# Gate products of a hybrid mixer layer: latent and context tokens side by side in one operand tile

## The chip, the cores and the metric

The kernel runs on one core of a Trainium2 chip. The metric is device time in microseconds (us) of one execution. TensorE (PE in the profile) multiplies, VectorE (DVE), ScalarE (ACT) and GpSimd (POOL) do the elementwise work, and SyncE (SP) issues most of the transfers. Each engine works through its own instructions in a fixed order.

## The reference

One layer over 256 latent tokens x, with 256 context tokens as a prefix. Both are normalised and modulated (hx, hc) and multiplied by parts of `w_in`:

```python
hc = modulate(rms_norm(h_ctx, norm1_g[l]), mc[0], mc[1])
out_c, s_f, s_b = token_mixer(hc, *mix_args, zero_state, zero_state, not last)
hx = modulate(rms_norm(x, norm1_g[l]), sh1, sc1)
out_x, _, _ = token_mixer(hx, *mix_args, s_f, s_b, True)
x = x + g1 * out_x
x = x + g2 * conv_ffn(modulate(rms_norm(x, norm2_g[l]), sh2, sc2), ...)
return rms_norm(x, final_g)
```

With one layer the context serves only to give the recurrence its starting states s_f and s_b, so of its projections only the gates (zf, zb) and the values v are needed. The latent tokens need the gates, q, v and all other columns: g, the three parts of the short convolution, and the two merging gates. D is 2048, there are 8 heads of 128 channels, and the FFN is 5632 wide. All is float32.

## The kernel before, in words

**Products.** Each float32 operand is split into an upper part and the remainder: `w_hi` (ScalarE) and `w_lo` (VectorE) for the weights, and two planes `[.., 0, :]` (upper) and `[.., 1, :]` (lower) of a tile for the tokens. A product is the sum of three matmuls: low weights by upper tokens, upper weights by upper tokens, upper weights by lower tokens (`mm3`, L117). The latent tokens are in `hx` [128, 16, 2, 256] and the context tokens in `hc`, of the same shape. Where only latent tokens are wanted (`proj`), one matmul of 512 columns moves upper and lower tokens at once, and one of 256 columns multiplies the low weights: 32 + 32 per call with one group of 256 output columns. Where both token sets are wanted (`block_products` with accumulators zacc, `proj_xc` and `proj_xc1` with accumulators acx), `mm3` is called once for hx and once for hc, in 256 columns each, so six matmuls per weight tile and k. zacc are seven accumulators and acx nine, each over 16 k.

**Weights' way.** A chunk of up to 1 MB comes by SyncE's queue into one of four `raw` slots (`wload`). It is split by halves into `w_hi` and `w_lo` (`wsplit`), five buffers each. `h_block` writes hx and hc for two k at a time; the first stage has eight such blocks with products as soon as they are written.

**Order of the work.** The program is written in one sequence; a scheduler places each engine's instructions ahead of time and may move independent work between. What it can move is limited by memory: a tile waits until those that lay in its place are done. After the first stage come four pairs of heads (g = 0 to 3). For each, gates and q, and then `hgrn` (L445 on): logarithms, scans on VectorE, transposes into kdt (L482), the starting state ps0, scores ps over eight levels (each with exponentials on ScalarE, products on VectorE, matmuls on TensorE and a masked copy), then po, the norm with pn, a reciprocal r (L581), and o_n (L582). While a pair's recurrence runs, TensorE works on other products. Accumulators of 512 columns take PSUM pairs of a pool with three buffers (`bank_pair`, psW); those of hgrn come from another with two (psH). A projection's pair is free again when `joined` has copied one half (ScalarE) and added the other (VectorE) into u, z or sg.

**Memory.** hx lies on the left, hc on the right. The recurrence's pools (vp, gp, g2) are on the left. When the gates are done, hc is released (L613), and its place on the right goes to map_ (the modulation accumulator `macc`) and tp (u, z, cv, sg of the projections that follow). Then mg, y_a and y_b come on the left. The following loop over j has four projections each, with `pump`: one chunk of `w_mod` into a raw slot and a multiply-add into macc (L636), which began with a memset on POOL (L632) and a small load of b_mod (L633).

Later stages: the gated merge into mg, `w_o`, the second norm, the FFN (`w_up`, depthwise convolution, `w_down`) and the final norm, all with products from hx or mg.

Of the kernel before, what the change touches and what calls it, by code (L numbers as in the profile page):

```python
# [16 lines left out]
P = 128  # L17
T = 256
# [18 lines left out]
def hybrid_layer_kernel(ctx: ExitStack, tc: tile.TileContext, I, out, dbg=None):  # L37
# [13 lines left out]
    lop = ctx.enter_context(tc.tile_pool(name="lop", bufs=5))  # L51
    hxp = ctx.enter_context(tc.tile_pool(name="hxp", bufs=1))
# [26 lines left out]

    behind_of = []  # L80

    def wsplit(parts, widths=(1024, 1024), raw=None):

        if raw is None:
            raw = wload(parts)
        for i, n in enumerate(widths):
            half = raw[:, 1024 * i:1024 * i + n]
            hi = hip.tile([P, 1024], F32R, name="w_hi", tag="w_hi")
            lo = lop.tile([P, 1024], F32R, name="w_lo", tag="w_lo")
            with ExitStack() as behind:  # L90
                after, sub = behind_of.pop(0) if behind_of else ((), nc.vector)
                for ins in after:
                    behind.enter_context(tc.issue_after(ins.ins))
                nc.scalar.activation(hi[:, :n], half, AF.Copy)  # L94
                sub.tensor_tensor(out=lo[:, :n], in0=half, in1=hi[:, :n].bitcast(F32), op=ALU.subtract)  # L95
            yield hi, lo

    def wviews(parts, kt):

        for i, (hi, lo) in enumerate(wsplit(parts)):  # L100
            hv = hi[:].rearrange("p (k n) -> p k n", k=kt // 2)
            lv = lo[:].rearrange("p (k n) -> p k n", k=kt // 2)
            for k in range(kt // 2):
                yield i * (kt // 2) + k, hv[:, k, :], lv[:, k, :]
# [4 lines left out]
    def split(dst, src):  # L109
        nc.scalar.activation(dst[0], src, AF.Copy)  # L110
        nc.vector.tensor_tensor(out=dst[1], in0=src, in1=dst[0].bitcast(F32), op=ALU.subtract)  # L111
# [106 lines left out]
    junk = hx[:, 0:2].rearrange("p a b c -> p (a b c)")  # L218
# [51 lines left out]
    def load_block(b):  # L270
        return wload([wblock(w_in, b * 256, 2, (1 + d) * AW, (512, 384)[d]) for d in range(2)])
# [4 lines left out]
    def h_block(b, pm):  # L276

        ks = slice(2 * b, 2 * b + 2)
        sm = stp.tile([P, 2, 256], F32, name="sm", tag="sm")
        copied = nc.vector.tensor_copy(sm[:], pm[:])  # L280
        pc = pm[:, 0, 0:8].rearrange("p (s i c) -> p s i c", s=2, i=2)
        for seg in range(2):
            for i in range(2):
                summed = mm(pc[:, seg, i, :], sm[:, seg, i * P:i * P + P], sel[:], seg == 0 and i == 0, seg == 1 and i == 1)
        pair = [[1, 2], [0, 2]]
        nc.vector.tensor_tensor(out=shcol[:, ks, :], in0=pc[:, 0], in1=strided(pb[:], 2 * b, pair), op=ALU.add)
        nc.vector.tensor_tensor(out=gcol[:, ks, :], in0=pc[:, 1], in1=strided(b1[:], 2 * b, pair), op=ALU.add)
        nc.vector.tensor_tensor(out=gcol[:, ks, :], in0=gcol[:, ks, :], in1=strided(pa[:], 32 + 2 * b, pair), op=ALU.mult)
        for i, h in enumerate((hx, hc)):
            ht = stp.tile([P, 2, T], F32, name="ht", tag=f"ht{i}")  # L290
            for k in range(2):
                kk = 2 * b + k
                nc.vector.tensor_scalar(out=ht[:, k, :], in0=xsT[:, kk, 2 * i:2 * i + 2, :].rearrange("p a b -> p (a b)"),
                                        scalar1=gcol[:, kk, i:i + 1], scalar2=shcol[:, kk, i:i + 1], op0=ALU.mult, op1=ALU.add)
            split((h[:, ks, 0, :], h[:, ks, 1, :]), ht[:])
        return copied, summed

    def block_products(b, halves):

        for d, (hi, lo) in enumerate(halves):  # L300
            for n in ((0, 1, 2, 3), (2, 0, 1))[d]:
                for k in range(2):
                    kk = 2 * b + k
                    at = (512, 384)[d] * k + n * P
                    ns = slice(at, at + P)
                    for i, h in enumerate((hx, hc)):
                        mm3(zacc[d, n][:, i, :], lo[:, ns], hi[:, ns], h[:, kk, 1, :], h[:, kk, 0, :], kk == 0 and i == 0, kk == KD - 1)
                yield
# [51 lines left out]
    dump("hc", hc[:].bitcast(F32))  # L360
# [5 lines left out]
    def proj(w, cols, src, kt):  # L366

        accs = [bank_pair("acc") for _ in cols]  # L370
        for c in range(kt // 8):
            for acc, c0 in zip(accs, cols):
                part = list(wviews([wblock(w, c * 1024, 8, c0, 256)], 8))
                for turn in range(2):
                    for k, hv, lv in part:
                        first = c == 0 and turn == 0 and k == 0
                        last = 8 * (c + 1) == kt and turn == 1 and k == 7
                        for n in range(2):
                            if wide_next[0] == (turn == 0):
                                mm(acc[:, n], hv[:, n * P:n * P + P], src[:, 8 * c + k], first, last)  # L380
                            else:
                                mm(acc[:, n, T:2 * T], lv[:, n * P:n * P + P], src[:, 8 * c + k, 0, :], first, last)
                wide_next[0] = not wide_next[0]
        return [acc[:].rearrange("p n (s t) -> p n s t", s=2) for acc in accs]

    def proj_xc(w, cols):
# [3 lines left out]
        for c in range(2):  # L390
            for n, (hi, lo) in enumerate(wsplit([wblock(w, c * 1024, 8, c0, P) for c0 in cols])):
                for k in range(8):
                    kk = 8 * c + k
                    for i, h in enumerate((hx, hc)):
                        mm3(accs[n][:, i, :], lo[:, k * P:k * P + P], hi[:, k * P:k * P + P],
                            h[:, kk, 1, :], h[:, kk, 0, :], kk == 0 and i == 0, kk == KD - 1)
        return accs

    def proj_xc1(w, c0):

        acc = bank_pair("acx")[:, 0].rearrange("p (a b) -> p a b", a=2)
        for k, hv, lv in wviews([wblock(w, 0, KD, c0, P)], KD):
            for i, h in enumerate((hx, hc)):
                mm3(acc[:, i, :], lv, hv, h[:, k, 1, :], h[:, k, 0, :], k == 0 and i == 0, k == KD - 1)
# [24 lines left out]
    def values(cb):  # L429
        pairs = [bank_pair("vacc") for _ in range(2)]  # L430
        accs = [pairs[t // 2][:, t % 2] for t in range(4)]
        for c4 in range(4):
            for k, hv, lv in wviews([wblock(w_in, c4 * 512, 4, 3 * AW + cb * 512, 512)], 4):
                kk = 4 * c4 + k
                for t in range(4):
                    h = hx if t < 2 else hc
                    ts = slice((t % 2) * P, (t % 2) * P + P)
                    mm(accs[t], h[:, kk, 0, ts], hv, kk == 0, False)
                    mm(accs[t], h[:, kk, 0, ts], lv, False, False)
                    mm(accs[t], h[:, kk, 1, ts], hv, False, kk == KD - 1)  # L440
# [3 lines left out]
    def hgrn(g, ft, q):  # L444
# [131 lines left out]
        split((oh[:], ol[:]), osq[:])  # L576
# [52 lines left out]
    def mod_steps():  # L629
        for seg in (4, 3, 2, 5):  # L630
            acc = map_.tile([P, D], F32, name="macc", tag="macc")
# [15 lines left out]
            else:  # L647
                yield
                bc = xp.tile([P, D], F32, name="bc", tag="bc")
                for c, (hi, lo) in enumerate(wsplit(None, raw=acc)):  # L650
                    for n in range(2):
                        cs = slice(n * 512, n * 512 + 512)
                        pm = psH.tile([P, 512], F32, name="pm2", tag="psh")
                        mm(pm[:], ones_r[:], hi[:, cs], True, False)
                        mm(pm[:], ones_r[:], lo[:, cs], False, True)
# [10 lines left out]
    for j in range(4):  # L666
# [19 lines left out]
        split((y_b[:, 2 * j:2 * j + 2, 0, :], y_b[:, 2 * j:2 * j + 2, 1, :]), cv[:])  # L686
# [8 lines left out]
        split((y_a[:, 2 * j:2 * j + 2, 0, :], y_a[:, 2 * j:2 * j + 2, 1, :]), sg[:])  # L695
# [7 lines left out]
    for j in range(8):  # L703
# [13 lines left out]
        split((mg[:, 2 * j:2 * j + 2, 0, :], mg[:, 2 * j:2 * j + 2, 1, :]), mb[0][:])  # L717
# [120 lines left out]
    with tc.manual_schedule(engines={nc.vector.engine}):  # L838
        for k2 in range(KD // 2 + 1):
            if k2 < KD // 2:  # L840
                ks = slice(2 * k2, 2 * k2 + 2)
                nc.vector.tensor_tensor(out=xg[:, ks, :], in0=xg[:, ks, :], in1=rbv, op=ALU.mult)
                for k in range(2 * k2, 2 * k2 + 2):
                    h2_hi[k2] = nc.scalar.activation(hx[:, k, 0, :], xg[:, k, :], AF.Identity, bias=sh2[:, k:k + 1])
            if k2 > 0:
                for k in range(2 * k2 - 2, 2 * k2):
                    h2_lo[k2 - 1] = nc.vector.scalar_tensor_tensor(out=hx[:, k, 1, :], in0=xg[:, k, :], scalar=sh2[:, k:k + 1], in1=hx[:, k, 0, :].bitcast(F32),  # L847
# [5 lines left out]
    mgp_cm.__exit__(None, None, None)  # L853
    onp.__exit__(None, None, None)

# [43 lines left out]
    fg = map_.tile([P, D], F32, name="fg", tag="macc")  # L899
    nc.scalar.dma_start(fg[:], I["final_g"].rearrange("(o d) -> o d", o=1).to_broadcast([P, D]))  # L900

    def y_part(k0):
        ys = hx[:, k0 % KD:k0 % KD + 2]
        split((ys[:, :, 0, :], ys[:, :, 1, :]), y[:, k0:k0 + 2, :])
        return lambda k, p: ys[:, k, p, :]
# [57 lines left out]
```

## Time and profile before

| what | value |
|---|---|
| runs, median (lowest to highest) | 1749.36 us (1749.27 to 1750.08), three runs |
| the profiled execution | 1748.87 us |
| its span, first to last instruction | 1747.1 us |
| mean granted TensorE clock | 0.993 |
| transferred | 384.95 MB, 220 GB/s mean |

The span is the profiled execution without its start and end. In the chain of waits a row gives start, duration, engine, output name and the hardware's count of passes; a float32 matmul that isn't split counts more than one pass, so that 8 ps instructions stand there as 16. In the grouped view a row gives busy time and mean of one in ns; matmuls overlap in the array, so such a mean is longer than the distance between two of them.

### The profile page before, as it was taken

The numbers are of one execution on the slowest core, as the hardware profiler recorded it, in microseconds if no ns is written. First come the engines' busy times: TensorE is split into PE (matmuls) and PEld (weight loads), VectorE is DVE, ScalarE is ACT, GpSimd is POOL, SyncE is SP. The second block draws the span as 40 slices with busy tenths as digits, with TensorE's granted clock in tenths as the row PEclk, the third lists the DMA queues.
The fourth block names the chain that finished last, engine by engine and source line by source line (L and its number), as shares of the span: only waits on it lengthen the run. The fifth ranks groups of instructions, "written<-read, shape, count | busy, mean of one in ns | idle before, by whom it ended". The sixth has DMA issues, their size and how long they took to land.

```text
span 1747.1 us, 25679 instructions
## 1 busy us (share of the span) xinstructions
PE 1712.9 (98%) x10391; PEld 1490.8 (85%) x10391; DVE 1311.7 (75%) x1689; ACT 894.8 (51%) x1141; POOL 20.5 (1%) x26
## 2 busy tenths in 40 slices
PE   5999999999999999999999999999999999999997
PEld 3778888999888888888888788888888888888886
DVE  4437267677998978878875589888888887876774
ACT  4217246565665544444465454444444454765653
POOL 0000000000000000000000000000000000000000
PEclk9999999999999999999999999999999999999999
DMA  9997323232877879989886367777777765656652
GB/s 333 346 331 231 97 73 98 74 120 93 272 258 246 273 266 324 318 275 314 289 304 218 125 199 246 234 235 237 241 241 239 234 202 193 193 193 193 193 193 72
DMA packets 288987, 384.95 MB, mean 220 GB/s; under 512 B 7812, under 2 KB 241581, under 8 KB 280038
## 3 DMA queue, kind: packets, MB, share of 16 engines
q1 hardware_dynamic: 287872, 379.82, 65.8%
q10 hardware_dynamic: 694, 3.24, 0.5%
q8 instruction: 81, 1.33, 0.3%
q14 instruction: 36, 0.29, 0.1%
q0 software_dynamic: 304, 0.26, 0.1%
HBM read 381.20 MB, written 2.10 MB: 219 GB/s over the span
## 4 chain that ended last, share of the span: by engine, by line
PE 97%; DVE 1%; ACT 1%; DMA 0%; issue 0%; SPq 0%; ACTq 0%
PE acc L114 56%; PE to L114 19%; PE acx L114 6%; PE vacc L114 5%; PE zacc L114 5%; PE pm L114 2%; PE ps L114 2%; PE po L114 1%; PE pt L236 1%; DMA xt<-in_x_dram 0%; PE pc L114 0%; DVE w_lo L95 0%; PE kdt L482 0%; ACT sq L789 0%; PE ptx L827 0%
## 5 line engine op out<-in xcount | busy, mean ns | idle before, releaser
L95 DVE TENSOR_TENSOR w_lo<-raw,w_hi 128x1024 fp32r<-128x1024 f32 (+1 forms) x521 | 630.0, 1218 | 226.1 <-ACT w_hi L94 210.4
L94 ACT ACTIVATE w_hi<-raw 128x1024 fp32r<-128x1024 f32 (+1 forms) x522 | 548.0, 1054 | 482.6 <-PE acc L114 316.8
L114 PE MATMUL acc<-hx,w_hi 128*128 128x512 f32 x2560 | 606.3, 392 | 2.3 <-DVE hx L847 2.3
L114 PEld LDWEIGHTS acc<-hx,w_hi 128*128 128x128 f32 x2560 | 476.7, 189 | 98.7 <-DVE hx L847 3.3
L114 PEld LDWEIGHTS acc<-hx,w_lo 128*128 128x128 f32 x2560 | 320.8, 192 | 8.1 <-DVE w_lo L95 0.8
L114 PE MATMUL acc<-hx,w_lo 128*128 128x256 f32 x2560 | 324.7, 283 | 0.1
L114 PE MATMUL to<-w_hi,hx 128*128 128x512 f32 (+1 forms) x792 | 221.5, 365 | 0.0
L636 DVE SCALAR_TENSOR_TENSOR macc<-raw,cst,macc 128x2048 f32<-128x2048 f32 x64 | 150.3, 2348 | 24.2 <-DMA raw<-in_w_mod_dram 18.5
L114 PEld LDWEIGHTS to<-w_hi,hx 128*128 128x128 f32 x792 | 142.8, 188 | 24.4
L114 PE MATMUL to<-w_lo,hx 128*128 128x512 f32 (+1 forms) x396 | 144.9, 366 | 0.0
L882 DVE SCALAR_TENSOR_TENSOR cvf<-av,pf,cvf 128x189 f32<-128x189 f32 (+2 forms) x352 | 129.2, 428 | 1.4 <-ACT cvf L870 1.3
L110 ACT ACTIVATE hx<-y 128x512 fp32r<-128x512 f32 x88 | 55.0, 630 | 87.6 <-PE to L114 86.1
L111 DVE TENSOR_TENSOR hx<-y,hx 128x512 fp32r<-128x512 f32 x88 | 60.7, 692 | 36.7 <-ACT hx L110 36.6
L114 PEld LDWEIGHTS to<-w_lo,hx 128*128 128x128 f32 x396 | 74.6, 188 | 12.2
L114 PE MATMUL to<-w_hi,mg 128*128 128x512 f32 (+1 forms) x288 | 81.1, 367 | 0.0
L114 PE MATMUL acx<-hx,w_hi 128*128 128x256 f32 x288 | 59.7, 286 | 0.0
L114 PEld LDWEIGHTS to<-w_hi,mg 128*128 128x128 f32 x288 | 51.8, 188 | 8.8
L114 PE MATMUL acx<-hc,w_hi 128*128 128x256 f32 x288 | 59.2, 285 | 0.0
L114 PE MATMUL to<-w_lo,mg 128*128 128x512 f32 (+1 forms) x144 | 52.7, 366 | 0.0
L114 PE MATMUL zacc<-hx,w_hi 128*128 128x256 f32 x224 | 49.3, 286 | 0.5 <-DVE hx L111 0.5
L114 PE MATMUL zacc<-hc,w_hi 128*128 128x256 f32 x224 | 47.1, 287 | 0.0
L114 PEld LDWEIGHTS acx<-hx,w_hi 128*128 128x128 f32 x288 | 45.3, 191 | 0.9
(240 smaller groups left out, 1758.6 us busy)
## 6 DMA issues: line engine op xcount, KB each, us to landing
raw<-in_w_up_dram SPq DMA_DIRECT2D x88, 1024.0 KB, 5.2
raw<-in_w_in_dram SPq DMA_DIRECT2D x81, 1024.0 KB, 5.9
raw<-in_w_mod_dram SPq DMA_DIRECT2D x64, 1024.0 KB, 6.7
raw<-in_w_down_dram SPq DMA_DIRECT2D x44, 1024.0 KB, 5.1
raw<-in_w_mod_dram SPq DMA_DIRECT2D x64, 512.0 KB, 6.9
raw<-in_w_o_dram SPq DMA_DIRECT2D x16, 1024.0 KB, 6.1
raw<-in_w_in_dram SPq DMA_DIRECT2D x24, 512.0 KB, 4.4
raw<-in_w_pa_dram SPq DMA_DIRECT2D x8, 1024.0 KB, 5.6
```

Source lines behind the costliest of these rows:

```text
L94: nc.scalar.activation(hi[:, :n], half, AF.Copy)
L95: sub.tensor_tensor(out=lo[:, :n], in0=half, in1=hi[:, :n].bitcast(F32), op=ALU.subtract)
L110: nc.scalar.activation(dst[0], src, AF.Copy)
L111: nc.vector.tensor_tensor(out=dst[1], in0=src, in1=dst[0].bitcast(F32), op=ALU.subtract)
L114: return nc.tensor.matmul(o, lhsT, rhs, start=start, stop=stop, skip_group_check=True)
L236: nc.tensor.transpose(pt[:, k, :], xts[2 * i + t][k4 // 2][:, kk * P:kk * P + P], ident[:])
L636: nc.vector.scalar_tensor_tensor(out=acc[:], in0=raw[:], scalar=cst[:, k, 0:1], in1=acc[:], op0=ALU.mult, op1=ALU.add)
L882: nc.vector.scalar_tensor_tensor(out=c4[:, ro, co], in0=a4[:, ri, ci], scalar=pf[:, tap * NF + f:tap * NF + f + 1], in1=c4[:, ro, co], op0 ...
```

## The change

hx and hc become one tile H [128, 16, 4, 256] with the planes latent low, latent upper, context upper, context low. The upper parts lie side by side (planes 1 and 2) and the lower at the ends (0 and 3). `mm3` takes both token sets at once: two matmuls over planes 1:3, and one over planes 0:4:3, of 512 columns each. hx is now a name for planes 0:2, so latent-only products use the same memory, upper and lower exchanged.

```diff
-    hx = hxp.tile([P, KD, 2, T], F32R)
-
-    hcp_cm = tc.tile_pool(name="hcp", bufs=1, side="right")
-    hcp = hcp_cm.__enter__()
-    hc = hcp.tile([P, KD, 2, T], F32R)
+    H = hp.tile([P, KD, 4, T], F32R)
+    hx = H[:, :, 0:2, :]
...
-    def mm3(o, wl, wh, sl, sh, start, stop):
-
-        mm(o, wl, sh, start, False)
-        mm(o, wh, sh, False, False)
-        mm(o, wh, sl, False, stop)
+    def mm3(o, wl, wh, k, start, stop):
+
+
+        mm(o, wh, H[:, k, 1:3, :], start, False)
+        mm(o, wh, H[:, k, 0:4:3, :], False, False)
+        mm(o, wl, H[:, k, 1:3, :], False, stop)
...
-                    for i, h in enumerate((hx, hc)):
-                        mm3(accs[n][:, i, :], lo[:, k * P:k * P + P], hi[:, k * P:k * P + P],
-                            h[:, kk, 1, :], h[:, kk, 0, :], kk == 0 and i == 0, kk == KD - 1)
+                    mm3(accs[n], part(1, k * P, k * P + P), part(0, k * P, k * P + P), kk, kk == 0, kk == KD - 1)
...
-    hcp_cm.__exit__(None, None, None)
-    map_ = ctx.enter_context(tc.tile_pool(name="map", bufs=1, side="right", reuse_waits="tile"))
+    map_cm = tc.tile_pool(name="map", bufs=1, reuse_waits="tile")
+    map_ = map_cm.__enter__()
     tp_cm = tc.tile_pool(name="tp", bufs=2, side="right", reuse_waits="tile")
     tp = tp_cm.__enter__()
-    mgp_cm = tc.tile_pool(name="mgp", bufs=1, reuse_waits="tile")
-    mgp = mgp_cm.__enter__()
...
-    mg = mgp.tile([P, KD, 2, T], F32R)
+    mg = H[:, :, 2:4, :]
...
+    lop_cm.__exit__(None, None, None)
+    lo_ring += range(KD // 2)
```

What else it moves: mg, which held its own memory, takes the context's planes of H. The pool of low weight halves is released before the FFN; from then on the low halves lie in eight places of H's planes 2 and 3 (`lo_half`). map_ moves to the left, and tp remains on the right, where hc no longer was; the last modulation row and final_g get other tiles. Everything that read hx or hc is rewritten for H.

TensorE's order at the recurrence of head pair 3. Before, from its transposes (kdt) on; ps are the scores, acc the mixer's projections:

```order
1538 L482 MATMUL kdt<-ident,ft 128x128 x8
1539 L114 MATMUL acc<-hx,w_hi 128x512 x20
1540 L114 MATMUL ps_3997<-v,gc 128x128 x8
1541 L114 MATMUL ps<-q,ks 64x64 x8
1542 L114 MATMUL acc<-hx,w_hi 128x512
1543 L114 MATMUL acc<-hx,w_lo 128x256 x28
1544 L114 MATMUL ps<-qe,ke 64x64 x8
1545 L114 MATMUL acc<-hx,w_lo 128x256 x4
1546 L114 MATMUL acc<-hx,w_hi 128x512 x19
1547 L114 MATMUL ps<-qe,ke 64x64 x8
1548 L114 MATMUL acc<-hx,w_hi 128x512 x13
1549 L114 MATMUL acc<-hx,w_lo 128x256 x32
```

It goes on in this way up to pn. Now, from the same transposes on:

```order
926 L491 MATMUL kdt<-ident,ft 128x128 x8
927 L126 MATMUL acc<-H,w_lo 128x256 x4
928 L126 MATMUL acc<-H,w_hi 128x512 x16
929 L126 MATMUL ps_3225<-v,gc 128x128 x8
930 L126 MATMUL ps<-q,ks 64x64 x8
931 L126 MATMUL ps<-qe,ke 64x64 x56
932 L126 MATMUL ps<-qe,ke 128x128 x4
933 L126 MATMUL po<-ft,kt 128x256 x2
934 L126 MATMUL po<-ft,v 128x256 x2
937 L126 MATMUL pn<-oh,ones_r 128x512
938 L126 MATMUL pn<-ol,ones_r 128x512
939 L126 MATMUL acc<-H,w_hi 128x512 x16
```

The projections that stood between the levels now stand behind pn.

VectorE's order around u, the first tile of the mixer's projections (its add frees the first PSUM pair). Before, with the logarithms of head pair 3 (X, gc) still ahead of its scans:

```order
361 L462 TENSOR_TENSOR X_3966<-X_3966,ft_3434 128x1024
362 L463 TENSOR_TENSOR gc_3967<-gc_3967,ft_3434 128x1024
363 L426 TENSOR_TENSOR q_3954<-q_3954,sq_3957 128x512
364 L95 TENSOR_TENSOR w_lo_4351<-raw_4344,w_hi_4350 128x1024
365 L125 TENSOR_TENSOR u_4292<-acc_4207,u_4292 128x512
366 L95 TENSOR_TENSOR w_lo_4404<-raw_4401,w_hi_4403 128x1024
```

Now, with the last step of head pair 3 (ft, ol, r, o_n) and the first two chunks of macc:

```order
416 L572 TENSOR_TENSOR ft_2854<-ft_2854,q_3182 128x512 x2
417 L123 TENSOR_TENSOR ol_3405<-osq_3401,oh_3404 128x512
418 L590 RECIPROCAL r_3410<-r_3410 128x512
419 L644 SCALAR_TENSOR_TENSOR macc_3518<-raw_3521,cst_91,macc_3518 128x2048
420 L591 TENSOR_TENSOR o_n_1101<-po_3392,r_3410 128x512
421 L644 SCALAR_TENSOR_TENSOR macc_3518<-raw_3620,cst_91,macc_3518 128x2048
422 L138 TENSOR_TENSOR u_3515<-acc_3430,u_3515 128x512
423 L138 TENSOR_TENSOR z_3609<-acc_3524,z_3609 128x512
```

u's add went from ahead of head pair 3's scans to behind its o_n.

More of the change, by code (lines that the diff above doesn't have):

```diff
@@ L77, in wload, with lo_half @@
         return raw
+    lo_ring = []
+    def lo_half():
+        if not lo_ring:
+            return lop.tile([P, 1024], F32R, name="w_lo", tag="w_lo")[:].rearrange("p (a n) -> p a n", a=2)
+        i = lo_ring.pop(0)
+        lo_ring.append(i)
+        return H[:, 2 * i:2 * i + 2, 2:4, :].rearrange("p a b t -> p a (b t)")
     behind_of = []
@@ L86, in wsplit @@
         for i, n in enumerate(widths):
-            half = raw[:, 1024 * i:1024 * i + n]
-            hi = hip.tile([P, 1024], F32R, name="w_hi", tag="w_hi")
-            lo = lop.tile([P, 1024], F32R, name="w_lo", tag="w_lo")
+            two = lambda ap: ap.rearrange("p (a n) -> p a n", a=2)[:, :, :n // 2]
+            half = two(raw[:, 1024 * i:1024 * i + 1024])
+            hi = two(hip.tile([P, 1024], F32R, name="w_hi", tag="w_hi")[:])
+            lo = lo_half()[:, :, :n // 2]
             with ExitStack() as behind:
@@ L217, in hybrid_layer_kernel @@
     rstd = sp.tile([P, 4], F32)
[L218 removed]
+    junk = H[:, 0].rearrange("p b c -> p (b c)")
     for i in range(2):
@@ L270, in load_block @@
     def load_block(b):
-        return wload([wblock(w_in, b * 256, 2, (1 + d) * AW, (512, 384)[d]) for d in range(2)])
+        raw = rawp.tile([P, 2, 2, 512], F32, name="raw", tag="raw")
+        for d, n in enumerate((512, 384)):
+            nc.sync.dma_start(raw[:, d, :, :n], wblock(w_in, b * 256, 2, (1 + d) * AW, n)[0])
+        return raw[:].rearrange("p d k n -> p (d k n)")
     def split_block(raw):
@@ L303, in block_products @@
                     kk = 2 * b + k
[L304 to L307, printed above, removed]
+                    at = 512 * k + n * P
+                    mm3(zacc[d, n], part(1, at, at + P), part(0, at, at + P), kk, kk == 0, kk == KD - 1)
                 yield
@@ L381, in proj @@
                             else:
-                                mm(acc[:, n, T:2 * T], lv[:, n * P:n * P + P], src[:, 8 * c + k, 0, :], first, last)
+                                mm(acc[:, n, 0:T], lv[:, n * P:n * P + P], src[:, 8 * c + k, 1, :], first, last)
                 wide_next[0] = not wide_next[0]
@@ L402, in proj_xc1 @@
         for k, hv, lv in wviews([wblock(w, 0, KD, c0, P)], KD):
-            for i, h in enumerate((hx, hc)):
-                mm3(acc[:, i, :], lv, hv, h[:, k, 1, :], h[:, k, 0, :], k == 0 and i == 0, k == KD - 1)
+            mm3(acc, lv, hv, k, k == 0, k == KD - 1)
         return acc
@@ L630, in mod_steps @@
         for seg in (4, 3, 2, 5):
-            acc = map_.tile([P, D], F32, name="macc", tag="macc")
+            acc = map_.tile([P, D], F32, name="macc", tag="macc") if seg != 5 else xp.tile([P, D], F32, name="bc", tag="bc")
             nc.gpsimd.memset(acc[:], 0.0)
@@ L648, in mod_steps @@
                 yield
-                bc = xp.tile([P, D], F32, name="bc", tag="bc")
-                for c, (hi, lo) in enumerate(wsplit(None, raw=acc)):
+                bc = xp.tile([P, D], F32, name="bc", tag="bc") if seg != 5 else acc
+                for c, part in enumerate(wsplit(None, raw=acc)):
                     for n in range(2):
-                        cs = slice(n * 512, n * 512 + 512)
                         pm = psH.tile([P, 512], F32, name="pm2", tag="psh")
-                        mm(pm[:], ones_r[:], hi[:, cs], True, False)
-                        mm(pm[:], ones_r[:], lo[:, cs], False, True)
+                        mm(pm[:], ones_r[:], part(0, n * 512, n * 512 + 512), True, False)
+                        mm(pm[:], ones_r[:], part(1, n * 512, n * 512 + 512), False, True)
                         nc.scalar.copy(bc[:, c * 1024 + n * 512:c * 1024 + n * 512 + 512], pm[:])
```

61 lines of the change are left out of this document (30 added, 31 removed).

## The prediction

> **What bounds the kernel now.** I read the page first: the engine totals, the chain that ended last, the groups.
>
> ```profile
> span 1747.1 us, 25679 instructions
> PE 1712.9 (98%) x10391; PEld 1490.8 (85%) x10391; DVE 1311.7 (75%) x1689; ACT 894.8 (51%) x1141; POOL 20.5 (1%) x26
> PE 97%; DVE 1%; ACT 1%; DMA 0%; issue 0%; SPq 0%; ACTq 0%
> L114 PE MATMUL acx<-hx,w_hi 128*128 128x256 f32 x288 | 59.7, 286 | 0.0
> L114 PE MATMUL zacc<-hx,w_hi 128*128 128x256 f32 x224 | 49.3, 286 | 0.5 <-DVE hx L111 0.5
> ```
>
> TensorE is the bound from end to end. So time can only be won by giving it less to do, and anything that leaves it without work is added to the span. The 98% is an average, so next comes the stretch that the change touches, in the chain of waits: the heads' recurrences (kdt, ps, po, pn) with what runs between.
>
> ```profile
> 168.14 43.52 PE vacc L114 x192
> 338.44 12.84 PE acx L114 x107
> 374.05 0.87 PE kdt L482 x8
> 378.04 2.40 PE ps L114 x32
> 383.51 1.08 PE ps L114 x32
> 389.82 0.62 PE ps L114 x16
> 405.14 0.62 PE ps L114 x16
> 407.50 0.89 PE ps L114 x8
> 411.81 3.02 PE po L114 x14
> 414.83 4.66 PE acx L114 x39
> 421.98 43.36 PE acc L114 x251
> 465.34 0.87 PE kdt L482 x8
> 548.25 3.46 PE po L114 x16
> 559.27 65.78 PE acc L114 x380
> ```
>
> The columns are start, duration, work. Each recurrence is a long serial pass over VectorE with scraps of TensorE work; from kdt (374.05) to the end of po (414.83) head pair 2 takes 40.8 us. TensorE loses nothing by it, because products of other tiles (acx there, acc at head pair 3, from 465.34 on) lie in between.
>
> **The merge itself.** A matmul's duration in the groups (286 ns) overlaps its neighbours'; what counts is the pace. 256 columns: 12.84 us / 107 = 120 ns. 512 columns: 43.52 / 192 = 227 ns. One product over both token sets in place of two saves 2 x 120 - 227 = 13 ns. With w_lo half as many again as w_hi's 288 and 224 for hx alone, there are 432 pairs in acx and 336 in zacc: 5.7 and 4.5 us, 10.2 at most. The Trainium skill's "TensorE: Matmul & The Clock Gate", section "Back-to-back issue gap", gives N / 2.4 + 2.5 ns for a warm matmul, so a fixed cost of only 2.5 ns per matmul: by it the 768 pairs would be worth 2 us, an estimate from that page. The trace's fixed part is five times that, and the trace decides.
>
> For acx I take the whole 5.7 us. For zacc not:
>
> ```profile
> 36.00:157.00 121.00, 120.31 (x957) 94.26 (x958) 50.18 (x99) 32.14 (x42) 0.95 (x1) 0.99 1.00 324
> GB/s 333 346 331 231 97 73 98 74 120 93 272 258 246 273 266 324 318 275 314 289 304 218 125 199 246 234 235 237 241 241 239 234 202 193 193 193 193 193 193 72
> ```
>
> In this stage (us, then PE, PEld, DVE, ACT, POOL busy, clock, DMA share, GB/s) the DMA share is 1.00 too. Its best slice moved 346 GB/s, so 121 us x 324 / 346 = 113 us is the least for the same bytes, and a TensorE gain can be had in part. Also, in the last block VectorE now has three w_lo and the copy of pf ahead of the shift and scale columns on which the last products wait (before, two w_lo, further on). Between 0 and 4.5 I take 3.0, nearer the PE row since TensorE is busy 120.3 of the 121 us.
>
> The low part is now read with stride (two runs of 256 columns). The nearest row of a strided operand is pm's, whose 512 columns are two runs of 256 of raw; the contiguous neighbour is po:
>
> ```profile
> 62.02 0.99 PE pm L114 x8
> ```
>
> Po took 3.46 us for 16 passes of 256 columns, 216 ns each, so 432 for 512; pm's eight passes (four 32-wide groups beside each other, so two in a row) took 0.99, at most 495 with all their overhead. So I price the stride at nothing; its other end, half rate, is a rival below.
>
> **The cover that goes.** H takes the place of hx and hc, and hc's memory on the right, freed once the gates were done, is no longer where u, z and macc are put: they now lie over memory that the recurrence's own pools hold until head pair 3 is finished. The order shown with the change has the result. Before, u of the first mixer projection was added up ahead of head pair 3's kdt:
>
> ```profile
> L125 DVE TENSOR_TENSOR u<-acc,u x4: 686/692/693, 447.3 to 592.4; 128x512 f32<-128x512 f32 x4
> ```
>
> (the first at 447.3, kdt at 465.34), so its PSUM pair came free and eight projections flowed between the levels. Now u stands behind r, macc, o_n and macc of the end of head pair 3; three projections fill the three PSUM pairs, the fourth has no bank, and TensorE's row from kdt on is 20 acc, 76 ps, 8 po, 2 pn and nothing between. Everything behind that fourth projection waits.
>
> How long? From the start of kdt:
> 1. To the end of po: 40.8 us in head pair 2. Only VectorE and ScalarE work counts in it, less what they did for others:
>
> ```profile
> 374.00:415.00 41.00, 22.71 (x79) 14.89 (x78) 6.09 (x5) 0.00 (x0) 1.00 0.24 78
> 415.00:465.00 50.00, 21.32 (x146) 19.51 (x145) 19.38 (x16) 0.00 (x0) 1.00 0.64 215
> ```
>
> (tile w_lo alone: PE, PEld, DVE, POOL). Five w_lo, 6.1 us, give a lower end of 34.7. Four w_lo stay in after's row, behind two weight loads that get a raw slot late, as the w_mod chunks keep three of the four; I take 38, ends 34.7 and 40.8.
>
> 2. From po to the restart, by the rows after head pair 2's po (ACT, then DVE):
>
> ```profile
> 414.93 0.60 ACT L572 ACTIVATE osq<-po 128x512 f32<-128x512 f32 x1 [5.91 <-PE po L114]
> 417.81 0.63 ACT L110 ACTIVATE oh<-osq 128x512 fp32r<-128x512 f32 x1
> 419.41 1.28 ACT L580 ACT_TABLE_LOAD   x1
> 420.71 0.69 ACT L580 ACTIVATE r<-pn,eps_t 128x512 f32<-128x512 f32 x1
> 418.48 0.69 DVE L111 TENSOR_TENSOR ol<-osq,oh 128x512 fp32r<-128x512 f32 x1
> 421.43 3.35 DVE L581 RECIPROCAL r<-r 128x512 f32<-128x512 f32 x1 [0.78 <-ACT r L580]
> 426.65 0.68 DVE L582 TENSOR_TENSOR o_n<-po,r 128x512 f32<-128x512 f32 x1
> 427.25 2.34 DVE L636 SCALAR_TENSOR_TENSOR macc<-raw,cst,macc 128x2048 f32<-128x2048 f32 x1
> ```
>
> 0.60 + 0.63 + 0.69 + two pn 0.46 + table 1.28 + root 0.69 = 4.35 (less where the table load is early), reciprocal 3.35, macc 2.34, o_n 0.68, macc 2.34, u 0.69: 13.7; I take 13.5. Ends 12.5 and 16, the latter with the 9.95 us that lay between po's end and the reciprocal's in the trace. Macc's own new wait hides in it: its memset on POOL now waits for po too, and
>
> ```profile
> L632 POOL MEMSET macc<- 128x2048 f32 x4 | 7.2, 1807 | 480.9 <-PE pc L114 334.3 <-DVE w_lo L95 133.3 <-PE acx L114 13.3
> macc<-in_b_mod_dram POOLq DMA_DIRECT2D x4, 8.0 KB, 1.8
> ```
>
> 1.8 + 1.8 us end well ahead of the reciprocal, 7.5 us behind po. Were it later, u would follow it one for one.
>
> 3. TensorE's own work in this time: kdt 0.87, 20 acc (4 x 0.120 + 16 x 0.227 = 4.1), ps 2.40 + 1.08 + 5 x 0.62 + 0.89 = 7.5, po 3.5, pn 0.5: 16.4 us. So it stands idle 38 + 13.5 - 16.4 = 35.1 us.
>
> Around the hole three smaller terms:
> - Ahead of kdt. From po of pair 2 on, TensorE now has 99 acc of 256 and 96 of 512 columns, 33.7 us, with po and pn 37, up to a kdt that VectorE must have ready.
>
> ```profile
> 415.00:466.00 51.00, 51.00 (x317) 45.94 (x315) 47.49 (x49) 37.26 (x41) 2.34 (x2) 1.00 0.65 218
> ```
>
> Of VectorE's 47.49 us there, 16 w_lo (19.38, quoted above) and a macc were for others: 25.8 without. After's row has 11 w_lo (1.22 each) in this piece: 39. TensorE waits 2 to 5 us; I take 3.
> - The clock. Where TensorE is idle at times, its granted clock falls:
>
> ```profile
> 990.00:998.00 8.00, 6.56 (x44) 5.45 (x42) 3.69 (x11) 3.08 (x11) 0.00 (x0) 1.00 0.00 0
> 998.00:1008.00 10.00, 7.64 (x22) 5.23 (x22) 9.65 (x17) 9.51 (x17) 0.00 (x0) 0.50 0.32 105
> ```
>
> Behind the second norm it was 0.50 for ten us. In the hole that doubles po, 3.5 us on the chain (a level's ps lies beside VectorE's next level), and some us of products after the restart. I take 4, ends 0 and 8. The Trainium skill's "TensorE: Matmul & The Clock Gate", Part 1, has the clock halved after about 3.4 us of idling and full again after as long of work; by it the restart would cost half of 3.4 us, an estimate from that page. The rows agree on the half, but not on the time: ten us there, in which TensorE had work for 7.6.
> - Changes between acc and ps, po that no longer happen: from 466.21 to 559.27 lie 79.7 us of acc by the paces above (233 of 512, 224 of 256 columns) and 11.5 of ps, po and pn, so 1.8 us went to the changes: -1.8.
>
> The rest of TensorE's row (w_o, the FFN, w_down) is in the same order as before; the low halves' places in H have more room than the pool that they replace, and mg's move touches no wait of TensorE. Those edits I cost at nothing; TensorE's back-to-back products cover them, and a late low half would cost at most its 1.22 us at each place. The gate products, being shorter, cover less of the levels of pairs 1 and 2: 0 to 3 us, I take 0.
>
> **Sum.** 35.1 + 3 + 4 - 1.8 = 40.3 lost, 5.7 + 3.0 = 8.7 won. The profiled run took 1748.87 us (1.8 of it outside the span), so 1748.87 + 40.3 - 8.7 = 1780.5; the median of the runs, 1749.36, is 0.5 above that run. Forecast: 1780 us.
>
> **The rivals.**
> - *The cover is kept (faster).* Then only the merge counts: 1748.9 - 8.7 = 1740. It needs u, z and macc free before head pair 3 ends, or other work in TensorE's row. For it: in head pairs 1 and 2 the same recurrence costs TensorE nothing. Against it: engines work their rows in order, u is behind r in VectorE's, and the fourth projection's bank is behind u. It decides if the idle time is under 8.7 us; 16.4 us of work against a serial pass of over 34 leaves no such room. Chance 0.06.
> - *The strided operand runs at half rate.* 112 + 144 low products at 227 ns more would be 58 us on top: 1838. The pm row speaks against it. 0.04.
> - *The durations of the groups are paces.* 2 x 286 less a 512-column matmul's 392, the other reading of the same page, would be 180 ns for each of 768 pairs, 138 us: 1651. Against it, 107 matmuls took 12.84 us and not 30. 0.01.
> - *The merge does not pay and the hole is small*, so that nothing is seen (within 0.2%, 3.5 us, about what a measurement of this kernel tells from no change): 0.03.
>
> The forecast's own case has 0.86. Its range, by the terms' ends: at the low end 34.7 + 12.5 - 16.4 + 2 + 0 - 1.8 - 10.2, or +20.8: 1770. At the high end 40.8 + 16 - 16.4 + 5 + 8 - 5.7 + 3, or +50.7: 1800. Not all ends come together, and some of the chance lies below: 1765 to 1797. Faster 0.07, same 0.03, slower 0.90.
>
> **What would show it.** In the profile after: zacc and acx of 512 columns at 227 ns each, 336 and 432 of them; the first stage about 3 us shorter; from kdt of head pair 3 a stretch of some 50 us in which TensorE is busy for a third, its clock at 0.5, ended by the add into u, and acc from there on without gaps; the idle time before acc put down to VectorE. If that stretch is full of acc, or if u is added up ahead of r, the forecast is wrong; if the span has grown but the hole is under 25 us, the chain was mis-sized.

## The result and the profile after

The changed kernel takes 1780.92 us (median of 4 runs, 1779.8 to 1782.81), the kernel before 1749.72 us beside it; the ratio is 1.0177 with a 95% interval of 1.0159 to 1.0194. Slower, as forecast, by 31.2 us against 31 forecast. The profiled execution took 1780.26 us, its span 1778.5. From the page of the profile after:

```profile
span 1778.5 us, 24106 instructions
PE 1710.1 (96%) x9623; PEld 1454.0 (82%) x9623; DVE 1312.4 (74%) x1689; ACT 890.9 (50%) x1137; POOL 20.6 (1%) x26
PE 91%; DVE 3%; DMA 2%; ACT 2%; issue 1%; SPq 0%; ACTq 0%
```

768 matmuls fewer, and yet TensorE is busy for a smaller share: it now waits. The timeline of TensorE, from kdt of head pair 3 to the fourth projection of the mixer, shows where (start, duration, engine, line, operation, count, and in brackets the idle time before and what ended it):

```profile
459.02 1.04 PE L491 MATMUL kdt<-ident,ft 128*128 128x128 f32 x8
...
468.89 0.69 PE L126 MATMUL ps<-qe,ke 128*64 128x64 f32 x16 [0.52 <-DVE ke L546]
477.17 1.12 PE L126 MATMUL ps<-qe,ke 128*64 128x64 f32 x16 [7.60 <-DVE qe L540]
479.58 1.12 PE L126 MATMUL ps<-qe,ke 128*64 128x64 f32 x16 [1.28 <-DVE qe L540]
482.65 1.12 PE L126 MATMUL ps<-qe,ke 128*64 128x64 f32 x16 [1.95 <-DVE qe L540]
...
492.60 1.67 PE L126 MATMUL po<-ft,kt 128*128 128x256 f32 x4 [0.36 <-DVE ft L572]
...
495.83 1.03 PE L126 MATMUL po<-ft,v 128*128 128x256 f32 x4
498.26 0.49 PE L126 MATMUL pn<-oh,ones_r 128*128 128x512 f32 x1 [1.41 <-ACT oh L122]
...
509.29 2.93 PE L126 MATMUL acc<-H,w_hi 128*128 128x512 f32 x6 [9.79 <-DVE u L138]
```

From the second level on every ps waits for VectorE, and acc comes back only when u has been added up, 9.79 us after pn. The longest wait between levels, 7.60 us, holds a late weight chunk: ScalarE stands for it ahead of the exponentials of that level, and VectorE splits the chunk before it comes to the level's products. ScalarE's row:

```profile
471.44 2.00 ACT L107 ACTIVATE w_hi<-raw 128x1024 fp32r<-128x1024 f32 x2 [3.34 <-DMA raw<-in_w_in_dram]
```

VectorE's timeline ahead of the restart has the row that the order promised:

```profile
500.25 3.35 DVE L590 RECIPROCAL r<-r 128x512 f32<-128x512 f32 x1 [1.31 <-ACT r L589]
503.52 2.25 DVE L644 SCALAR_TENSOR_TENSOR macc<-raw,cst,macc 128x2048 f32<-128x2048 f32 x1
505.69 0.69 DVE L591 TENSOR_TENSOR o_n<-po,r 128x512 f32<-128x512 f32 x1
506.29 2.34 DVE L644 SCALAR_TENSOR_TENSOR macc<-raw,cst,macc 128x2048 f32<-128x2048 f32 x1
508.55 0.68 DVE L138 TENSOR_TENSOR u<-acc,u 128x512 f32<-128x512 f32 x1
```

Three windows of the kernel after (us; then PE, PEld, DVE, ACT, POOL busy; granted clock, DMA share, GB/s):

```profile
459.00:509.30 50.30, 22.16 (x201) 18.23 (x199) 34.06 (x46) 21.63 (x34) 2.33 (x2) 0.71 0.23 77
...
480.00:490.00 10.00, 4.07 (x62) 3.40 (x58) 9.85 (x19) 5.78 (x11) 0.00 (x0) 0.50 0.01 2
...
510.00:520.00 10.00, 10.00 (x52) 8.71 (x51) 9.85 (x9) 3.98 (x5) 0.00 (x0) 0.79 0.86 280
```

In 50.3 us TensorE is busy for 22.2, some of it at half the clock. Before, it was busy all of that time; 50.3 us from kdt on:

```profile
465.34:515.64 50.30, 50.30 (x370) 43.95 (x369) 48.04 (x57) 30.06 (x40) 0.00 (x0) 1.00 0.72 245
```

To see the rest of the account, take the distance from the start of each matmul to the start of the next, and add it up by the name of the output (this divides TensorE's whole time, waits and slow clock included; us):

```
            before     after   difference
ps           29.99     50.94       +20.95
pn            1.85     12.42       +10.57
po           12.31     14.33        +2.02
pm           46.26     49.26        +3.00
pt           20.20     22.44        +2.24
acx         107.61    102.24        -5.37
zacc         87.06     83.51        -3.55
acc         987.99    988.28        +0.29
ptx, vacc, rb, pc, kdt (sum)        +1.06
first to last start                +31.2
```

The hole stands in ps, pn and po: 33.5 us. acx brought what the pace promised. zacc brought 3.55. pm (the modulation's products, between the blocks of zacc) and pt (transposes; the last four stand ahead of the last block's products, so that a wait of 1.62 us for H counts as theirs) took 5.2 back.

### The profile page after: what moved, and what is told of

It is laid out like the page before. It is cut to its first block, busy times and chain, and to the rows that moved or that the text cites. A ratio compares the mean times of both kernels' runs of the same rounds, so it can differ in the third digit from the quotient of the medians.

```text
span 1778.5 us, 24106 instructions
## 1 busy us (share of the span) xinstructions
PE 1710.1 (96%) x9623; PEld 1454.0 (82%) x9623; DVE 1312.4 (74%) x1689; ACT 890.9 (50%) x1137; POOL 20.6 (1%) x26
## 4 chain that ended last, share of the span: by engine, by line
PE 91%; DVE 3%; DMA 2%; ACT 2%; issue 1%; SPq 0%; ACTq 0%
PE acc L126 53%; PE to L126 18%; PE acx L126 6%; PE vacc L126 5%; PE zacc L126 4%; PE pm L126 2%; DMA raw<-in_w_in_dram 1%; PE ps L126 1%; PE po L126 1%; DVE w_lo L108 1%; PE pt L248 1%; DMA xt<-in_x_dram 0%; ACT w_hi L107 0%; PE pc L126 0%; DMA raw<-in_w_mod_dram 0%
## 5 line engine op out<-in xcount | busy, mean ns | idle before, releaser
L126 PE MATMUL acc<-H,w_hi 128*128 128x512 f32 x2560 | 605.3, 393 | 12.1 <-DVE u L138 9.8
L126 PEld LDWEIGHTS acc<-H,w_hi 128*128 128x128 f32 x2560 | 478.7, 190 | 109.6 <-DVE u L138 10.1
L108 DVE TENSOR_TENSOR w_lo<-raw,w_hi 128x1024 fp32r<-128x1024 f32 (+1 forms) x258 | 308.5, 1211 | 146.1 <-ACT w_hi L107 141.7
L108 DVE TENSOR_TENSOR H<-raw,w_hi 128x1024 fp32r<-128x1024 f32 x263 | 319.4, 1220 | 70.7 <-ACT w_hi L107 70.2
L126 PE MATMUL to<-w_hi,H 128*128 128x512 f32 (+1 forms) x1080 | 302.6, 366 | 0.0
L126 PEld LDWEIGHTS to<-w_hi,H 128*128 128x128 f32 x1080 | 194.6, 188 | 33.2
L126 PEld LDWEIGHTS acc<-H 128*128 128x128 f32 x1408 | 175.4, 191 | 5.3 <-DVE H L108 1.6
L126 PE MATMUL acc<-H 128*128 128x256 f32 x1408 | 176.9, 283 | 0.6 <-DVE H L108 0.6
L126 PE MATMUL acc<-H,w_lo 128*128 128x256 f32 x1152 | 146.8, 283 | 0.0
L126 PE MATMUL to<-H 128*128 128x512 f32 (+1 forms) x396 | 144.9, 366 | 0.0
```

Source lines behind the costliest of these rows:

```text
L108: sub.tensor_tensor(out=lo, in0=half, in1=hi.bitcast(F32), op=ALU.subtract)
L126: return nc.tensor.matmul(o, lhsT, rhs, start=start, stop=stop, skip_group_check=True)
```

## The experiments

The theory: the slowdown is the lost cover. u and z lie over memory of the recurrence, so three PSUM pairs fill up and TensorE has nothing to do until head pair 3 is done. Rival 1: the merge itself takes the cover, since shorter gate products leave less to put between the levels. Rival 2: chunks of w_mod, which wait for macc in the raw slots, starve the weights.

**1. late_uz: the wait without the merge.** In the kernel before, only this is added (for u and the first two z, at j = 0):

```diff
-        joined(u[:], pc0)
+        with ExitStack() as late:
+            if j == 0:
+                late.enter_context(tc.issue_after(last_on.ins))
+            joined(u[:], pc0)
```

> The kernel before, gate products unmerged, hx and hc apart; only the adds into u and the first two z are issued behind the last o_n of head pair 3. Theory (the hole comes from the late u and z, not from the merge): TensorE again stands without work from kdt of head pair 3 to the add into u; 50 us less 14 to 16 of its own work gives about 34 us more, 1784 us (1777 to 1790). Rival 1 (the merge itself takes the cover, since shorter gate products leave less to put between the levels): nothing is merged here, so 1750. Rival 2 (the chunks of w_mod hold the raw slots and starve the weights): the accumulator is as free as before, so 1750 to 1755.

Measured: 1778.16 us, ratio 1.0161 (1.0147 to 1.0175). TensorE's window from kdt to the restart, and the restart in its timeline:

```profile
465.50:507.80 42.30, 20.65 (x188) 16.88 (x186) 30.89 (x44) 18.85 (x30) 0.00 (x0) 0.72 0.28 96
```

```profile
507.84 5.50 PE L114 MATMUL acc<-hx,w_hi 128*128 128x512 f32 x16 [5.56 <-DVE u L125]
```

Without any merge the same hole appears, and 27.8 of the 31.2 us with it. It is at the low edge of what was expected for two reasons: no macc stands ahead of u here (5.56 us of idling behind pn in place of 9.79), and the way from kdt to the end of po is 34.3 us in place of 37.9. Rival 1 falls as the cause, and a late u and z are enough.

**2. defer_macc: the chunks of w_mod later.** The changed kernel with

```diff
-        pump(1)
+        pump((0, 2, 1, 1)[j])
```

at all four places of the loop over j.

> The changed kernel with the first four chunks of w_mod put two iterations' worth later (none at j = 0, two at a time at j = 1), so that no macc stands ahead of u on VectorE and no raw slot is held by w_mod in the recurrence. Theory: the hole stays, since u and z still lie over the recurrence's memory; its tail loses two macc (4.7 us) and the 7.6 us that a level waited for a weight load can shrink: 1769 to 1776. Rival 2 (w_mod's raw slots are the cause): most of the 34 us goes, 1745 to 1752. Rival 1 (the merge): 1781.

Measured: 1774.09 us, ratio 1.0136 (1.0122 to 1.015): 6.8 us less than the change. kdt is at 458.74 and the restart at 504.44, 45.7 us in place of 50.3. Behind pn nothing is won, however. TensorE's restart, and VectorE ahead of it:

```profile
504.44 6.45 PE L126 MATMUL acc<-H,w_hi 128*128 128x512 f32 x16 [9.80 <-DVE u L138]
```

```profile
501.44 2.34 DVE L644 SCALAR_TENSOR_TENSOR macc<-raw,cst,macc 128x2048 f32<-128x2048 f32 x1
503.70 0.68 DVE L138 TENSOR_TENSOR u<-acc,u 128x512 f32<-128x512 f32 x1
```

Two macc are still ahead of u: the chunks of j = 1 are as early as that, once TensorE stands. So the edit didn't remove what I said that it would, and what it won lies elsewhere: the longest wait between levels is 3.08 us instead of 7.60.

```profile
471.86 0.78 PE L126 MATMUL ps<-qe,ke 128*64 128x64 f32 x16 [3.08 <-DVE qe L540]
```

The weight loads come earlier: SyncE has issued the last two ahead of the restart by 457.29, where in the change it does so from 457.19 to 466.64. Rival 2 is a part of the loss here, no more.

**3. split: the merge taken back inside the changed kernel.**

```diff
-        mm(o, wh, H[:, k, 1:3, :], start, False)
-        mm(o, wh, H[:, k, 0:4:3, :], False, False)
-        mm(o, wl, H[:, k, 1:3, :], False, stop)
+        for i, (hi, lo) in enumerate(((1, 0), (2, 3))):
+            mm(o[:, i, :], wh, H[:, k, hi, :], start and i == 0, False)
+            mm(o[:, i, :], wh, H[:, k, lo, :], False, False)
+            mm(o[:, i, :], wl, H[:, k, hi, :], False, stop)
```

> The changed kernel with each gate product made again as two of 256 columns, H and the placement of u, z and macc as changed. Theory: TensorE has the 5.7 us of acx back to do, the first stage is longer by up to 2 us, but the order now leaves 10 us of projections in the recurrence of head pair 3 instead of 4, so the sum hardly moves: 1778 to 1785. Rival 1 (the merge is the cause of the hole): 1750 to 1756.

Measured: 1778.16 us, ratio 1.0159 (1.0144 to 1.0175). The hole is there with unmerged products as well. The 6 us more of projections that lie in it and the 5.4 us of acx that come back nearly cancel: by the distances between starts, ps has 7.1 us less than in the change and acx 5.6 more; zacc has 5.2 more, and pm and pt have 4.9 less.

**4. cover_only and cover: memory that is free early.** u and z get the buffers of q and of gc, whose last readers are done early in the recurrence. These two leave gp for a pool `ge` on the right, opened ahead of the recurrence's pools and kept to the end of the merge.

```diff
-        q = gp.tile([P, 2, T], F32, name="q", tag="q", bufs=2)
+        q = ge.tile([P, 2, T], F32, name="q", tag="q", bufs=2)
...
-        gc = gp.tile([P, 2, 2, T], F32, name="gc", tag="gc")
+        gc = ge.tile([P, 2, 2, T], F32, name="gc", tag="gc")
...
+    zz = ge.tile([P, 2, 2, T], F32, name="z", tag="gc")
...
-        u = tp.tile([P, 2, T], F32, name="u", tag="u")
+        u = ge.tile([P, 2, T], F32, name="u", tag="q", bufs=2)
```

Each z is now one half of zz in turn. cover_only is this alone; cover has the later chunks of run 2 too.

> The changed kernel with u and z in the memory of q and gc, w_mod's chunks where the change has them. TensorE's order now has 14 us of projections between kdt and pn of head pair 3, where the change has 4 and the run with later chunks had 37. If both the memory and the raw slots held by w_mod count, in this order: 10 us of the hole are filled, then the weights are missing: 1768 to 1773, between the change and the covered run. If the memory alone were all: as the covered run, 1764. If w_mod's chunks alone were: as the change, 1781.

> The changed kernel, gate products merged, with u and z placed in memory that dies early in the recurrence (the buffers of q and of gc, now a pool of their own on the right) and w_mod's first chunks later as in the deferred run. From kdt to pn of head pair 3 about 37 us of projections lie in TensorE's order instead of 4. Theory: 25 to 34 us come back: 1747 to 1756. Rival 1 (the merge is the cause): 1781, or 1769 to 1776 by the later chunks. Rival 2: as in the deferred run, no better than it.

Measured: cover_only 1774.83 us, ratio 1.0138 (1.0121 to 1.0155); cover 1763.96 us, ratio 1.0078 (1.0065 to 1.0091). The memory alone brings 6 us, the later chunks alone 7, both 17 (each beside the kernel before that was measured with it: 7.9, 7.5 and 17.6). Both fell short of what was expected. TensorE's timeline, first of cover_only, then of cover, says why:

```profile
514.75 5.65 PE L126 MATMUL acc<-H,w_hi 128*128 128x512 f32 x16 [12.60 <-ACT w_hi L107]
```

```profile
525.69 5.71 PE L126 MATMUL acc<-H,w_hi 128*128 128x512 f32 x16 [12.80 <-ACT w_hi L107]
```

Not u, but w_hi ends this wait. SyncE's timeline in cover has two chunks of w_mod from 461.86 on and two more from 487.16, which makes four for four slots, and no weight chunk until 519.20, when the first macc (516.92 to 519.17) has freed one:

```profile
461.86 3.35 SPq L76 DMA_DIRECT2D raw<-in_w_mod_dram  x2
472.82 7.74 SPq L76 DMA_DIRECT2D raw<-in_w_in_dram  x2
487.16 7.12 SPq L76 DMA_DIRECT2D raw<-in_w_mod_dram  x2
519.20 3.24 SPq L76 DMA_DIRECT2D raw<-in_w_in_dram  x2
```

So once u and z no longer hold TensorE, the mechanism of rival 2 is next in line: macc lies over v, which po reads last, and its chunks hold the slots. Between the levels in cover, TensorE has no idle time left.

**5. cover_later, cover_last, spread: where the chunks can go.** As cover, with (0, 0, 2, 2) chunks a projection in the four iterations, then (0, 0, 0, 4), then (0, 0, 0, 1) with the rest as three instead of two in the first six iterations of the merge.

> As the covered run, with w_mod's first eight chunks two iterations later instead of one (0, 0, 2, 2 chunks a projection in place of 0, 2, 1, 1), so that no raw slot is held by w_mod before the recurrence ends. Theory: the 12.8 us for which TensorE still waited for weights behind pn in the covered run go, and with them the slow clock behind it, and what is left is the merge: 1745 to 1750. Rival (that wait is the end of the recurrence itself, r and o_n, and the merged kernel can't be covered): 1760 to 1764.

> As cover_later, with all sixteen early chunks of w_mod in the last of the four iterations (0, 0, 0, 4 a projection), so that no multiply-add into macc stands ahead of the adds into z behind the recurrence. In cover_later TensorE still waited 2.9 us there for z and ran some 1.6 us at the slow clock. Theory: those 4.5 us go and the merge is seen at last: 1745 to 1748 beside a kernel before of 1750 to 1751. Rival (the merge gains nothing on the whole, what acx wins is lost elsewhere): 1750 to 1752.

> As cover_last, but w_mod's chunks neither early nor crowded: 0, 0, 0, 1 a projection in the four iterations, then three instead of two in the first six iterations of the gated merge, so that the sum at its end is the same. Theory: neither the 4.5 us of cover_later (z behind macc) nor the 14 us of cover_last (weights that came late in the crowded fourth iteration) are there, and the kernel is below the one before by what acx wins: 1744 to 1748, beside 1750 to 1751.

Measured: cover_later 1750.88 us, ratio 0.9999 (0.999 to 1.0008); cover_last 1761.74 us, 1.0063 (1.0049 to 1.0076); spread 1756.6 us, 1.0034 (1.0021 to 1.0046). cover_later has the whole loss back: the hole is closed and the kernel equals the one before, a little above the 1745 to 1750 that was expected. All that TensorE still waits for in it between 170 and 900 us is a z behind macc; TensorE, then VectorE:

```profile
533.75 5.49 PE L126 MATMUL acc<-H,w_hi 128*128 128x512 f32 x16 [2.92 <-DVE z L138]
```

```profile
528.07 2.35 DVE L653 SCALAR_TENSOR_TENSOR macc<-raw,cst,macc 128x2048 f32<-128x2048 f32 x1
...
532.92 0.68 DVE L138 TENSOR_TENSOR z<-acc,z 128x512 f32<-128x512 f32 x1
```

The next two runs removed this wait and missed all the same, by 14 and by 9 us over the top of what was expected: new waits stand where I put the chunks. TensorE's waits in cover_last between 600 and 665 us (total, times, longest):

```profile
PE acc L126 <- ACT w_hi L107: 7.6, 2, 5.9
PE pc L126 <- DVE macc L653: 3.7, 1, 3.7
```

The window of that stretch shows the transfers at 0.92 of their time:

```profile
605.00:660.00 55.00, 45.42 (x232) 39.44 (x231) 46.27 (x38) 18.93 (x24) 2.34 (x2) 0.84 0.92 326
```

And in spread, VectorE is busy for 149.80 of 170 us of the merge, with the transfers at 0.94 of their time, and TensorE for 164. Its largest wait there, in the first row, is for low halves of weights:

```profile
PE acc L126 <- DVE w_lo L108: 4.4, 2, 3.0
690.00:860.00 170.00, 164.08 (x925) 145.09 (x924) 149.80 (x122) 73.06 (x88) 2.29 (x2) 0.97 0.94 329
```

Before, from 600 to 860 us, the transfers were at 0.86 and TensorE never waited:

```profile
600.00:860.00 260.00, 260.00 (x1497) 230.41 (x1496) 209.52 (x184) 123.90 (x144) 4.61 (x4) 0.99 0.86 297
```

Before, chunks of w_mod came while the recurrence ran (SyncE issued eleven between 433 and 552 us). What is moved out of that time has to find room in stretches that have little; that the full transfers make these waits is my reading of the windows, which no run tests by itself.

**6. What the merge is worth under cover.** The merge taken back as in run 3, in all (cover_later_split, spread_split) or for zacc alone (cover_last_zsplit, spread_zsplit).

> As cover_later, with each gate product made again as two of 256 columns: the merge alone taken back, under full cover. By the pace of the rows (13 ns a pair) and a first stage that other things bound: 5 to 7 us more than cover_later. If zacc's pairs count in full too: 10 us more. If a pair is only worth 2.5 ns: 1 to 2 us more. If there is cost in the strided operand of the merged products: less than cover_later.

> As cover_last, with the products of the first stage (zacc) made again as two of 256 columns; acx stays merged. If the first stage is bound by its transfers and by the last block's columns, zacc's 5.4 us by the pace mostly turn into waits of pm for chunks of w_mod: 0 to 2 us more than cover_last. If TensorE bounds that stage: 4 to 5 us more.

> As spread, with the first stage's products (zacc) in two of 256 columns, acx merged. After the last pair of runs: zacc's merge is worth nothing on the whole, since pm's waits for w_mod and the last block's columns take its 5 us: within 2 us of spread, on either side.

> As spread, with zacc and acx both in two of 256 columns: the merge taken back under full cover and with nothing else late. Theory: acx's 5.4 us on top of spread_zsplit, 1750 to 1753. Rival (acx wins nothing either): as spread.

Measured, each beside its merged kernel, taken together with it: cover_later_split 1751.39 us, ratio 1.0008 (0.9999 to 1.0017), against 0.9999 merged; cover_last_zsplit 1759.14 against 1761.74; spread_zsplit 1759.7 and spread_split 1762.5 against 1756.6. None of the four came out as I expected. The differences have no common sign for zacc (2.6 us faster unmerged, 3.1 slower), and for all together are 0.5 and 5.9 us. These totals alone leave the worth of the merge open between nothing and 6 us, since weights that come a little late elsewhere move them as much. The traces are clearer. acx takes 102.2 us in every merged profile and 107.6 to 107.8 in every unmerged one. The first stage, by the start of vacc behind it, ends at 169.1 us in the mean of the seven profiles with merged zacc (167.76 to 170.14) and at 169.3 in the seven with two products of 256 columns (168.14 to 170.29): its merge is worth nothing that can be seen, though zacc itself shrank. (From the first zacc on, the stage is 1.2 us shorter in the mean with merged zacc, but that first zacc starts 1.0 us later.)

Under full cover acx's gain is lost again too. In cover_later_split TensorE waits for nothing between 170 and 900 us; in cover_later it waits the 2.92 us for z, and acc as a whole, by the distances between starts, takes 993.7 us where it took 988.7. These 5.0 us stand against the 5.6 us by which acx is shorter in this pair. No version was faster than the kernel before.

## Why the prediction was right

**The cause.** That u falls behind the end of head pair 3, that TensorE then stands without work, and that this outweighs the merge: shown by late_uz, which has the wait and not the merge, by split, which has the hole with unmerged products, and by cover_later, which has the merge and neither the hole nor the loss. The wait for u is not the whole of it: cover has no wait for u and still stands 12.80 us for weights, so the raw slots that w_mod holds must come free as well. No run has the chunks of cover_later without the memory of cover.

**The size of the hole.** From kdt to the end of po: 459.02 to 496.9, or 37.9 us, where I took 38. From there to the restart 12.4, where I took 13.5. With 16.4 of own work at full clock the hole costs 33.9 us, where I had 35.1. Macc's new wait hid behind the reciprocal, as said: its memset on POOL ended at 498.72, the reciprocal at 503.60.

**Ahead of kdt.** I had 3 us of idling; there was none. TensorE had all of the time from po to kdt filled, and VectorE had time to spare:

```profile
419.35:459.02 39.67, 39.67 (x232) 35.30 (x231) 32.68 (x38) 28.12 (x31) 0.00 (x0) 1.00 0.41 136
```

VectorE was busy for 32.7 us, with all eleven w_lo in it (two of them beside po), where I had counted 39; TensorE had 39.7 us of work where I had counted 37, since 17 more acc lie between the matmuls of po. The step that failed was the count of what both had to do there, of VectorE's other work above all.

**The clock.** The rows show 0.50 in the hole, but the 4 us were divided wrongly. po took 4.27 us instead of 3.46, and these 0.8 us are part of the 37.9; its doubling was wrong, since the granted clock was back at 1.00 from 494 on. At the restart, the distances between acc's matmuls add up to 2.4 us more than their pace (the first six of 512 columns took 2.93 us), with the clock at 0.50:

```profile
494.00:497.00 3.00, 2.85 (x14) 2.17 (x12) 0.00 (x0) 0.05 (x1) 0.08 (x1) 1.00 0.00 0
509.30:513.00 3.70, 3.70 (x9) 2.96 (x10) 3.70 (x4) 1.06 (x1) 0.00 (x0) 0.50 1.05 344
```

By the Trainium skill's "TensorE: Matmul & The Clock Gate", Part 1, half of 3.4 us would be lost there, 1.7, an estimate from that page. The trace has a little more.

**The merge.** The pace decided: acx went from 107.6 to 102.2 us, 5.4 us for 432 pairs, or 12.4 ns a pair where I had 13. One row of the chain after, all three matmuls of a product in it, the strided one too:

```profile
361.44 16.78 PE acx L126 x74
```

That is 227 ns each, so the stride cost nothing and the rivals of half rate and of 180 ns a pair are out. The estimate of 2.5 ns a pair is out for TensorE's own time. The section "Back-to-back issue gap" of the Trainium skill's "TensorE: Matmul & The Clock Gate" gives the formula behind it for the gap of an isolated matmul, and here matmuls stand in a stream, each with a weight load.

**The first stage.** This is the term that was wrong: 3.0 us won in the sum, 1.7 lost in the pair of profiles, and 0.2 won in the mean over 14. A block did become shorter, by 0.5 us, from 15.5 to 14.9 (pm of the chain, two rows before, then two after):

```profile
99.29 1.92 PE pm L114 x16
...
114.76 1.92 PE pm L114 x16
...
101.35 2.78 PE pm L126 x24
...
116.29 2.78 PE pm L126 x24
```

but the last block's products start later, at 149.81 in place of 147.62, behind more w_lo on VectorE. Its rows are, before:

```profile
144.61 2.35 DVE L95 TENSOR_TENSOR w_lo<-raw,w_hi 128x1024 fp32r<-128x1024 f32 x2
146.88 0.69 DVE L111 TENSOR_TENSOR hx<-ht,hx 128x512 fp32r<-128x512 f32 x1
```

and after:

```profile
142.90 1.23 DVE L108 TENSOR_TENSOR w_lo<-raw,w_hi 128x1024 fp32r<-128x1024 f32 x1 [0.69 <-ACT w_hi L107]
...
144.19 1.21 DVE L108 TENSOR_TENSOR w_lo<-raw,w_hi 128x1024 fp32r<-128x1024 f32 x1
...
147.34 1.21 DVE L108 TENSOR_TENSOR w_lo<-raw,w_hi 128x1024 fp32r<-128x1024 f32 x1
148.47 1.28 DVE L123 TENSOR_TENSOR H<-ht,H 128x512 fp32r<-128x512 f32 x2
```

and the low half of H, on which the products wait, comes last. I had named this and set it too low, beside a start of the stage that differs by some us from one profile to the next.

So the two sides were both too large, 40.3 lost where it was about 35, and 8.7 won where it was 3.7 in this pair of profiles, and the errors cancelled: that the total is closer than its terms is luck.

## What to carry to other kernels

A tile that is merged to save operations also merges lifetimes: ask what used to lie in the memory that is no longer freed, and which serial stage it covered. Such a hole can be sized beforehand, as the length of the chain without its cover, less the engine's own work in it, from rows of an earlier pass of the same chain that still has its cover. When the cover is mended, look for the next holder in line (here the slots of the weight loads), and when loads are moved out of a stage, ask whether they were using it.

## What had not been expected

The placement of the chunks of w_mod has hardly any slack. With the same cover, three places for the same sixteen chunks gave ratios of 0.9999, 1.0034 and 1.0063, a spread of 11 us, more than the whole merge could have won; the transfers took 0.92 and 0.94 of their time in the two stretches above, into which the chunks were moved.
